# A streaming-encoder trunk on one core: other pads in front of the operands of the products

## The chip, the cores and the metric

The kernel runs on one core of one Trainium2 chip. The metric is the device time of one execution in microseconds (us). The kernel before takes 1405.71 us (median of 3 runs, 1403.22 to 1407.08).

## The reference

Four pre-norm residual layers work on a sequence of 256 tokens of 1024 features. Each has a token mixer and a gated channel mixer; a final RMS norm ends the program.

```python
for i in range(DEPTH):                       # 4
    hn = rmsnorm(h, norm_mix[i])
    if i % 3 == 0:   mix = diff_attention(hn, ...)     # layers 0 and 3
    elif i % 3 == 1: mix = conformer_conv(hn, ...)     # layer 1
    else:            mix = gated_deltanet(hn, ...)     # layer 2
    h = h + mix
    h = h + conv_ffn(rmsnorm(h, norm_ffn[i]), ...)     # every layer
return rmsnorm(h, norm_final)
```

`conv_ffn` multiplies by a 1024 x 5632 matrix, runs a causal convolution of width 3 over the tokens, gates one half with the other, and multiplies by a 2816 x 1024 matrix. All inputs are float32.

## The kernel before

**Layout.** The residual `h` lies feature-major: 128 features of a block on the 128 partitions, 8 blocks of 256 tokens along each partition. All weights of the large products come through one stream, `wst`, in units of 128 x 1024 float32 (512 KB). `Stream.upto` (lines 158 to 178) loads a unit to `wraw` on SyncE's DMA queue, ScalarE casts it to `whi` (line 173) and VectorE puts the remainder into `wlo` (line 174). Both have 4 buffers of 4096 bytes per partition.

**A product in three parts.** A float32 product is made of three products of the faster type `float32r`: high times high, high times low and low times high. `mm3` (lines 282 to 284) and the same three calls in `pair_proj` (lines 298 to 300) issue them:

```python
pe.matmul(o, w[0], x[0], start=start, stop=False)   # L282  hi weights, hi activations
pe.matmul(o, w[0], x[1], start=False, stop=False)   # L283  hi weights, lo activations
pe.matmul(o, w[1], x[0], start=False, stop=stop)    # L284  lo weights, hi activations
```

The second argument is the stationary operand, which TensorE loads first (128 columns, 512 bytes of each partition); the third is the moving operand, streamed through (256 columns, 1024 bytes of each partition). Each product has its own weight load, which runs beside the product before it.

**Which products there are.** The projections of the normed activations move `xh`, `xl` (written in `norm_split`, lines 239 and 240; one block of 256 tokens per step over the 8 blocks): into `psu` in the channel mixers, `pqk` in the attention, `pcu` in the conformer, `pgc` in the delta net. The projections back to the residual move the split activations: `facth`, `factl` in the first three channel mixers, `oh`, `ol` in the attention, `cacth`, `cactl` in the conformer, `goh`, `gol` in the delta net; all go into `acc`. In three places the weights are the moving operand, 512 columns wide, and the activations the stationary one: `pv` (values of the attention), `pz` (gate of the delta net) and the last channel mixer's way back (`acc<-whi,facth`). One small product of the delta net, `pba`, has a stationary operand of 32 columns only (`wA`, `wB`), with `xh`, `xl` moving. Products of plain float32 (the taps of the conformer's convolution into `pcc` at line 712, transposes, the scan of the delta net) are made elsewhere.

**What sets the order.** The order of the work is written out by hand: `attn_order`, `gdn_order` and `ffn_order` list the steps, and the table `WAIT` says how many steps a side chain is put off.

**Where a tile lies.** Tile pools give out the memory of a partition one tile after another, so a tile's place depends on the sizes of those before it. `offset` (line 141) puts an unused tile, a pad of 32n bytes per partition, ahead of the next ones:

```python
def offset(pool, name, n):
    if n:
        pool.tile([P, 8 * n], F32, name="pad" + name, bufs=1)
```

It is called behind `h` in the pool `resid` (line 147, n = AT_X), behind the rope tables in the same pool (line 229, n = -AT_X % 4), in the pool `small` (line 1322, n = 1), and at the head of the pools of the channel mixer (line 397, AT_F), the attention (line 489, AT_A), the conformer (line 668, AT_C) and the delta net (line 818, AT_G). The numbers are

```python
AT_X, AT_F, AT_A, AT_C, AT_G = 3, 2, 1, 1, 1
```

The buffers of one name are whole multiples of 512 bytes apart, and so are the steps within them, so that one number, the place modulo 512 bytes, holds for all products of a kind.

Of the kernel before, what the change touches and what calls it, by code (L numbers as in the profile page):

```python
# [32 lines left out]
PE_TAPS_LAST = 11  # L33
POOL_TAPS = 6
LAG = 2
AT_X, AT_F, AT_A, AT_C, AT_G = 3, 2, 1, 1, 1
MAX_DIAGS = 88
DIAG_STEP = 4
TAIL = 4
# [86 lines left out]
def trunk(ctx: ExitStack, tc: tile.TileContext, xT, pos, wst, wba, params, consts, rows, lamp, nfin, out, layers=None):  # L126
# [5 lines left out]
    resid = ctx.enter_context(tc.tile_pool(name="resid", bufs=1))  # L132
    wpool = ctx.enter_context(tc.tile_pool(name="wpool", bufs=1))
    small = ctx.enter_context(tc.tile_pool(name="small", bufs=2))
# [6 lines left out]
# [4 lines that stand above are left out]
# [81 lines left out]
    rs_bc = resid.tile([P, S], F32, name="rs_bc")  # L226
    rs_tok = resid.tile([P, 32], F32, name="rs_tok")[:, 0:2]
    rope = [resid.tile([P, S], F32, name=f"rope{n}") for n in range(2)]
    offset(resid, "r", -AT_X % 4)
    state = {}  # L230

    def norm_bank(b, gname, goff):
# [1086 lines left out]
        nm, off = names(k + 1)  # L1319
        return lambda b: norm_bank(b, nm, off)  # L1320

    offset(small, "s", 1)
    warm = small.tile([P, P], F32, name="warm", tag="warm", bufs=1)
    ve.memset(warm, 0.0)
    ac.copy(small.tile([P, 1], F32, name="warm1", tag="warm1", bufs=1), warm[:, 0:1])
# [176 lines left out]
```

## Time and profile before

| what | value |
|---|---|
| median of 3 runs | 1405.71 us (1403.22 to 1407.08) |
| the profiled execution, its own time | 1403.77 us |
| its span, first to last instruction | 1401.9 us |
| TensorE busy with products | 1382.7 us, 99% of the span |
| TensorE busy with weight loads | 1311.3 us, 94% |
| VectorE, ScalarE, GpSimd busy | 79%, 63%, 7% |
| granted TensorE clock, mean | 0.997 |
| DMA | 223.94 MB, mean 160 GB/s |

A product's record lasts from when its first column enters to when the last result is out (about 0.28 us for 256 columns), and the next product begins long before that. So the records of neighbours overlap, and the engine's busy share says little. What a product costs is the step from its start to the start of the next one. It is read from the timeline, or by dividing a stretch that holds nothing else by the number of products in it.

### The profile page before, as it was taken

What the parts mean: (1) busy time and instruction counts of PE and PEld (TensorE: products, weight loads), DVE (VectorE), ACT (ScalarE), POOL (GpSimd) and SP (SyncE); (2) the same over time, 40 slices, a digit from 0 to 9 for tenths busy, and PEclk for the clock granted to TensorE, in tenths of its full rate; (3) what the DMA queues carried; (4) which work ended last, traced back from release to release, by engine and by line L of the source; (5) the groups of instructions that cost most, each with busy time, mean ns of one, the idle gap of its engine ahead of it and who ended that gap; (6) DMA issues with size and microseconds to landing.
All of it is one profiled execution on the core that took longest, in us unless ns stands there. A gap on an engine that the chain in (4) does not pass through costs nothing.

```text
span 1401.9 us, 27575 instructions
## 1 busy us (share of the span) xinstructions
PE 1382.7 (99%) x10868; PEld 1311.3 (94%) x10868; DVE 1112.5 (79%) x1994; ACT 877.4 (63%) x1621; POOL 94.1 (7%) x112
## 2 busy tenths in 40 slices
PE   9999999999999999999999999999999999999998
PEld 7889999999889999998998999999999988999996
DVE  7977877788988877787895786787778786887776
ACT  6668965566556555565747765665556576655554
POOL 0010000004530000000100011000000000000000
PEclk9999999999999999999999999999999999999999
DMA  8445666554325666654463333566665544566662
GB/s 278 146 121 165 181 182 183 186 180 129 91 61 170 193 183 183 185 177 133 123 192 93 122 91 121 157 184 187 184 182 180 181 127 134 162 196 185 190 181 91
DMA packets 63138, 223.94 MB, mean 160 GB/s; under 512 B 7200, under 2 KB 8736, under 8 KB 63008
## 3 DMA queue, kind: packets, MB, share of 16 engines
q1 hardware_dynamic: 62720, 221.65, 52.1%
q8 instruction: 85, 1.39, 0.4%
q10 hardware_dynamic: 288, 0.52, 0.1%
q14 instruction: 45, 0.37, 0.1%
HBM read 221.10 MB, written 1.05 MB: 158 GB/s over the span
## 4 chain that ended last, share of the span: by engine, by line
PE 87%; DVE 7%; ACT 3%; issue 1%; POOL 1%; DMA 0%; SPq 0%; POOLq 0%; ACTq 0%; DVEq 0%
PE psu L282 12%; PE psu L284 11%; PE psu L283 11%; PE acc L283 8%; PE acc L282 8%; PE acc L284 8%; PE pcc L712 3%; DVE wlo L174 2%; PE pgc L282 2%; PE pgc L283 2%; PE pgc L284 2%; ACT whi L173 1%; PE pz L282 1%; PE pz L284 1%; PE pz L283 1%
## 5 line engine op out<-in xcount | busy, mean ns | idle before, releaser
L173 ACT CAST whi<-wraw 128x1024 fp32r<-128x1024 f32 (+1 forms) x417 | 435.7, 1047 | 301.3 <-PE psu L283 118.1
L174 DVE TENSOR_TENSOR wlo<-wraw,whi 128x1024 fp32r<-128x1024 f32 (+1 forms) x417 | 509.1, 1222 | 140.9 <-ACT whi L173 132.7
L282 PE MATMUL psu<-xh,whi 128*128 128x256 f32 x1344 | 380.9, 283 | 0.0
L283 PE MATMUL psu<-xl,whi 128*128 128x256 f32 x1344 | 379.3, 282 | 0.0
L284 PE MATMUL psu<-xh,wlo 128*128 128x256 f32 x1344 | 377.2, 281 | 0.0
L284 PEld LDWEIGHTS psu<-xh,wlo 128*128 128x128 f32 x1344 | 255.0, 190 | 0.0
L283 PEld LDWEIGHTS psu<-xl,whi 128*128 128x128 f32 x1344 | 252.7, 188 | 0.3
L282 PEld LDWEIGHTS psu<-xh,whi 128*128 128x128 f32 x1344 | 251.6, 187 | 0.4
L283 PE MATMUL acc<-factl,whi 128*128 128x256 f32 x528 | 147.8, 280 | 0.0
L282 PE MATMUL acc<-facth,whi 128*128 128x256 f32 x528 | 147.5, 280 | 0.0
L284 PE MATMUL acc<-facth,wlo 128*128 128x256 f32 x528 | 146.9, 279 | 0.0
L426 DVE SCALAR_TENSOR_TENSOR fy<-fs,prm,fy 128x255 f32<-128x255 f32 (+1 forms) x352 | 146.4, 477 | 0.0
L422 ACT ACTIVATE fy<-fs,prm 128x256 f32<-128x256 f32 x176 | 96.4, 593 | 7.8 <-DVE fs L418 7.6
L282 PEld LDWEIGHTS acc<-facth,whi 128*128 128x128 f32 x528 | 99.2, 188 | 0.1
L283 PEld LDWEIGHTS acc<-factl,whi 128*128 128x128 f32 x528 | 99.1, 188 | 0.0
L284 PEld LDWEIGHTS acc<-facth,wlo 128*128 128x128 f32 x528 | 98.6, 187 | 0.0
L276 ACT CAST facth<-fa 128x256 fp32r<-128x256 f32 x88 | 35.6, 405 | 90.4 <-DVE fa L430 90.4
L418 DVE TENSOR_TENSOR fs<-psu,rs_bc 128x512 f32<-128x512 f32 x88 | 60.7, 690 | 36.5 <-PE psu L284 36.4
L282 PE MATMUL pqk<-xh,whi 128*128 128x256 f32 x256 | 73.4, 287 | 0.0
L284 PE MATMUL pqk<-xh,wlo 128*128 128x256 f32 x256 | 73.0, 285 | 0.3 <-DVE wlo L174 0.3
L283 PE MATMUL pqk<-xl,whi 128*128 128x256 f32 x256 | 72.9, 285 | 0.0
L282 PE MATMUL pgc<-xh,whi 128*128 128x256 f32 x240 | 69.0, 287 | 0.0
(352 smaller groups left out, 2872.8 us busy)
## 6 DMA issues: line engine op xcount, KB each, us to landing
wraw<-wst SPq DMA_DIRECT2D x415, 512.0 KB, 3.7
h<-xT SPq DMA_DIRECT2D x4, 256.0 KB, 5.4
prm<-params SPq DMA_DIRECT2D x1, 564.0 KB, 7.3
wraw<-wst SPq DMA_DIRECT2D x2, 256.0 KB, 4.3
gain<-nfin SPq DMA_DIRECT2D x1, 512.0 KB, 4.0
out<-fz SPq DMA_DIRECT2D x2, 256.0 KB, 2.0
out<-fz ACTq DMA_DIRECT2D x2, 256.0 KB, 2.5
cst<-consts SPq DMA_DIRECT2D x1, 264.0 KB, 7.0
```

Of the source, the lines that this page charges most:

```text
L173: ac.copy(hi[:, qs], src[:, qs])
L174: ve.tensor_tensor(lo[:, qs], src[:, qs], hi[:, qs].bitcast(F32), ALU.subtract)
L276: state["hi"] = ac.copy(hi, a)
L282: pe.matmul(o, w[0], x[0], start=start, stop=False)
L283: pe.matmul(o, w[0], x[1], start=False, stop=False)
L284: pe.matmul(o, w[1], x[0], start=False, stop=stop)
L418: ve.tensor_tensor(s, ps.rearrange("p (g t) -> p g t", g=2), bc(rs_bc, 2), ALU.mult)
L422: ac.activation(y[:, gv], s[:, gv], AF.Identity, scale=col("ffn_dw", c + 2), bias=col("ffn_dw_b", (i * NP_ + p) * 2 + gv))
L426: ve.scalar_tensor_tensor(y[:, gv, j:], s[:, gv, :S - j], col("ffn_dw", c + 2 - j), y[:, gv, j:], ALU.mult, ALU.add)
L712: pe.matmul(pc[:, 0:S], dg, u[:, j:j + S], start=(n == 0), stop=(n == npe - 1))
```

## The change

Nothing but the pads: their numbers, and two more of them get a name.

```diff
-AT_X, AT_F, AT_A, AT_C, AT_G = 3, 2, 1, 1, 1
+AT_X, AT_R, AT_S, AT_F, AT_A, AT_C, AT_G = 7, 3, 10, 0, 0, 4, 2
...
-    offset(resid, "r", -AT_X % 4)
+    offset(resid, "r", AT_R)
...
-    offset(small, "s", 1)
+    offset(small, "s", AT_S)
```

The instructions and their order on every engine stay as they are; only addresses differ. In the two programs as they are laid out, the operands lie at these places, in bytes modulo 512 within their partition:

| operand | before | after |
|---|---|---|
| `xh`, `xl` | 224 | 352 |
| `facth`, `factl` | 448 | 352 |
| `oh`, `ol` | 416 | 352 |
| `goh`, `gol` | 352 | 352 |
| `cacth`, `cactl` | 288 | 352 |
| weights `whi`, `wlo` | 384 | 64 |
| residual `h` | 128 | 128 |
| taps' input `cu` (three buffers) | 32, 160, 416 | 96, 224, 480 |

The distance "moving less stationary, modulo 512" of the products with 256 columns is thus, before, 352 for `xh` and `xl`, 64 for `fact`, 32 for `o`, 480 for `go`, 416 for `cact`; after, it is 288 for all of them. For the products that move the weights, 512 columns wide, it is 160 before (`pv`, `pz`) and 448 (`acc<-whi,facth`); after, it is 224 for both.

## Rows read from the trace of the kernel before

**Rows 1.** The page: busy us (share of the span), number of instructions.
```profile
PE 1382.7 (99%) x10868; PEld 1311.3 (94%) x10868; DVE 1112.5 (79%) x1994; ACT 877.4 (63%) x1621; POOL 94.1 (7%) x112
```
**Rows 2.** The page: chain that ended last, share of the span by engine.
```profile
PE 87%; DVE 7%; ACT 3%; issue 1%; POOL 1%; DMA 0%; SPq 0%; POOLq 0%; ACTq 0%; DVEq 0%
```
**Rows 3.** Waits of PE alone, longest sums: us in total, times, longest.
```profile
PE poT L621 <- ACT os L617: 2.7, 4, 0.9
PE pat L599 <- DVE pr L591: 1.7, 5, 0.4
```
**Rows 4.** A stretch of a channel mixer, all engines: busy us (count), PEclk, DMA share, GB/s.
```profile
275.41:298.45 23.04, 23.04 (x194) 23.04 (x193) 18.60 (x29) 13.35 (x21) 0.00 (x0) 1.00 0.55 184
```
**Rows 5.** The same stretch, PE on tile psu alone: us, PE busy (products), PEclk.
```profile
275.41:298.45 23.04, 23.04 (x192) 1.00 0.55 184
```
**Rows 6.** Five stretches, PE on tile acc: fact, o, o earlier, go, cact moving.
```profile
298.45:307.75 9.30, 9.30 (x79) 1.00 0.57 174
117.62:124.62 7.00, 7.00 (x62) 1.00 0.59 184
113.82:117.06 3.24, 3.24 (x29) 1.00 0.01 4
890.52:896.67 6.15, 6.15 (x54) 1.00 0.28 89
415.65:429.89 14.24, 14.24 (x122) 1.00 0.45 123
```
**Rows 7.** A stretch of the products with 32 weight columns, PE on tile pba.
```profile
635.73:637.77 2.04, 2.04 (x20) 1.00 0.36 32
```
**Rows 8.** Stretches of products that move 512 columns, PE on acc and pz.
```profile
1377.99:1386.15 8.16, 8.15 (x35) 1.00 0.00 1
...
701.47:712.69 11.22, 11.22 (x48) 1.00 0.63 200
```
**Rows 9.** PE's groups by line and form, one of three lines each: count, busy, mean ns.
```profile
L282 PE MATMUL psu<-xh,whi 128*128 128x256 f32 x1344 | 380.9, 283 | 0.0
...
L282 PE MATMUL acc<-facth,whi 128*128 128x256 f32 x528 | 147.5, 280 | 0.0
...
L282 PE MATMUL pqk<-xh,whi 128*128 128x256 f32 x256 | 73.4, 287 | 0.0
...
L282 PE MATMUL pgc<-xh,whi 128*128 128x256 f32 x240 | 69.0, 287 | 0.0
...
L282 PE MATMUL acc<-oh,whi 128*128 128x256 f32 x128 | 36.9, 291 | 0.0
L282 PE MATMUL acc<-goh,whi 128*128 128x256 f32 x128 | 36.7, 292 | 0.0
...
L282 PE MATMUL pcu<-xh,whi 128*128 128x256 f32 x112 | 32.7, 292 | 0.0
...
L298 PE MATMUL psu<-xh,whi 128*128 128x256 f32 x64 | 18.1, 283 | 0.0
...
L282 PE MATMUL acc<-cacth,whi 128*128 128x256 f32 x64 | 17.6, 283 | 0.0
```
**Rows 10.** The same view: products with 512 moving columns.
```profile
L282 PE MATMUL acc<-whi,facth 128*128 128x512 f32 x88 | 34.7, 396 | 0.0
...
L282 PE MATMUL pz<-whi,xh 128*128 128x512 f32 x64 | 27.0, 422 | 0.0
...
L282 PE MATMUL pv<-whi,xh 128*128 128x512 f32 x64 | 25.9, 412 | 0.3 <-ACT whi L173 0.3
```
**Rows 11.** The chain in order of time: start us, us, what; taps of the convolution.
```profile
339.92 4.33 PE pcc L712 x20
```
**Rows 12.** Timeline of PE in a channel mixer: start us, us, what.
```profile
207.07 0.28 PE L282 MATMUL psu<-xh,whi 128*128 128x256 f32 x1
207.20 0.28 PE L283 MATMUL psu<-xl,whi 128*128 128x256 f32 x1
```

## The prediction

> **What bounds the kernel now.** I begin with the page's busy shares: TensorE's products cover 99% of the span, no other engine more than 79% [rows 1]. A busy share alone proves little here, since the records overlap, so the chain of waits comes next: 87% of it is TensorE [rows 2]. Then the waits of TensorE alone: the longest sum is 2.7 us, the next 1.7 us [rows 3]. TensorE is hardly ever held up by anyone; the time is the sum of its steps, and every nanosecond off a step is off the end, as long as the others keep up. They do: in a stretch of a channel mixer VectorE, which is next, is busy 18.60 of 23.04 us, the DMA share is 0.55, and the clock is granted in full, its upper level of 2.4 GHz [rows 4]. TensorE's part would have to shrink by 19% there before VectorE ruled.
>
> What does a step cost? The stretch of `psu` holds 192 products in 23.04 us, which is 120.0 ns each [rows 5]. The same three-part product has other steps elsewhere. Windows that open in the middle of a run also count the two products still in flight (a record lasts 0.28 us [rows 12]), so two are taken off all of rows 6 but the first: `fact` 9.30/79 = 117.7 ns, `o` 7.00/60 = 116.7 ns, though `o` has an earlier stretch at 3.24/27 = 120.0 ns, `go` 6.15/52 = 118.3 ns, `cact` 14.24/120 = 118.7 ns [rows 6]. Code, sizes, clock and accumulators are alike; what differs between these kinds is the place of the moving operand. And with 32 weight columns instead of 128, but `xh` and `xl` moving from the same place as in `psu`, the step is 2.04/18 = 113.3 ns [rows 7]. So some 6.7 ns of `psu`'s 120.0 belong to the weight load that runs beside it: the two reads hinder each other, and how much depends on how they lie to each other. That is what the change touches.
>
> **The change, part by part.** No instruction is added, removed or moved; no wait and no queue changes. Costs arise only where a read is faster or slower from its new place.
>
> *Products that move `xh`, `xl`.* Three lines times (1344 + 64 + 256 + 240 + 112) = 6048 products [rows 9]; two groups of 16 per line are left out. Now 120.0 ns each, at distance 352. The new distance, 288, is in no row. Bounds: 113.3 ns below (the same stream with a quarter of the weights), 120.0 ns above, as no kind has a higher steady step. Which value? Three readings of the five kinds offer themselves. By the moving operand's own place the twin is `go`, already at 352: 118.3 ns. By the distance, if the pattern repeats every 256 bytes, the twin of 288 is 32, which is `o`: 116.7 ns. By the distance modulo 512 the nearest row is `xh` itself, 64 bytes away: 120.0 ns. The rows don't decide between the last two: by 256 the distances 32, 64, 96, 160, 224 give 116.7, 117.7, 120.0, 118.7, 118.3, by 512 the distances 32, 64, 352, 416, 480 give the same values in the same order, and both curves are smooth. Two readings of three say less than 120.0; I take the middle of the four kinds that aren't `xh`, 117.8 ns: 2.2 ns x 6048 = 13.3 us less.
>
> *Products that move `fact`, `o`, `go`, `cact`.* 1584, 384, 384 and 192 products [rows 9]. At 117.8 ns they change by +0.1, +1.1, -0.5 and -0.9 ns, which is +0.2, +0.4, -0.2, -0.2 us: nothing in sum. Bounds: all at 113.3 ns would take off 4.4 x 1584 + 3.4 x 384 + 5.0 x 384 + 5.4 x 192 = 11.2 us; all at 120.0 ns would add 2.3 x 1584 + 3.3 x 384 + 1.7 x 384 + 1.3 x 192 = 5.8 us.
>
> *Products that move 512 columns of weights.* 3 x (88 + 64 + 64) = 648 [rows 10]. The two distances they have now give 8.16/35 = 233.1 and 11.22/48 = 233.8 ns [rows 8], so place counts for 0.7 ns over them, 0.5 us in sum: nothing. Each holds one weight load like a product of half its length; were that load's share of 6.7 ns to vanish, 4.3 us would go.
>
> *Plain float32 products.* The taps stream 256 columns in 4.33/20 = 216 ns, though their input starts 4 bytes further at every tap [rows 11]: at this slower pace place is not felt. Nothing, either way.
>
> *Writers of the moved tiles.* ScalarE and VectorE write and read at other places too. If that cost them anything, VectorE's 19% of free time in rows 4 hides it.
>
> Sum: 13 us off the profiled execution's 1403.77 us gives 1390.5 us; its time lies 1.9 us under the median of the runs, well within their spread. I say **1390 us**. A difference under 0.3%, some 4.2 us, can't be told from none.
>
> **A rule against the change.** Row first: `psu` and `pba` move the same operand from the same place, and a shorter weight load makes the step 120.0 or 113.3 ns [rows 5, 7]. The Trainium skill's page "SBUF — State Buffer", section "Who interferes with whom", gives TensorE two independent read ports, one for the moving operand and one for the weight load, and says "PE and ACT never wait on anyone". By that rule where operands lie couldn't matter, and the time would stay at 1404 us. The trace disagrees with it as far as those rows go, so I leave it a small chance.
>
> **The rivals.**
>
> *Place is not the cause* (the change does nothing). The five steps could stem from the stages they stand in. For it: `o` has both 116.7 and 120.0 ns at one place [rows 6], so place alone does not fix the step; the start of a run does too. Against it: `psu` keeps 120.0 over 192 products while the `fact` products next to it, in the same stage with the same neighbours, keep 117.7 [rows 5, 6]. It gives 1404 us; 1 in 9.
>
> *The new place is nearly free of hindrance.* At 113.3 ns everything, `xh` gives 6.7 x 6048 = 40.5 us and the rest 11.2 us: 1352 us, or 1348 with the 512 columns. Two thirds of the way down, at 115.2 ns, `xh` gives 4.8 x 6048 = 29.0 us and the rest 2.5 x 1584 + 1.5 x 384 + 3.1 x 384 + 3.5 x 192 = 6.4 us: 1368 us. For it: the step has room down to rows 7, and among five kinds, laid out in five ways, the steps already spread over half of that room. Against it: none of them comes below 116.7. Chance 1 in 4 for anything under 1380 us.
>
> *Slower: all products take `xh`'s step.* The new distance, 288, lies 64 bytes from the worst one, 352, and far from the best ones, 32 and 64. If the pattern repeats every 512 bytes only and is smooth, `fact`, `o`, `go` and `cact` all move towards `xh`. It decides as soon as the step at 288 is above 119.5 ns: then `xh` gains nothing that pays for the 5.8 us that the others lose, and the time is 1410 us. Should the steps go beyond 120.0, each ns costs 6.0 us on `xh` and 2.5 us on the rest; single steps of 125 ns exist (0.13 us within a run whose mean is 120.0 [rows 12]), but no run keeps them. For it: plain nearness. Against it: that curve needs its peak and the fall to 117.7 at 64 in a part no row shows. Chance 1 in 4, most of it between 1408 and 1412 us.
>
> **How the numbers follow.** Forecast, a step of 116.7 to 118.7 ns: 0.39, between 1381 us (20.0 us on `xh`, 2.6 us on the rest) and 1398 us (7.9 us on `xh`, 2.5 us back from the rest). Nearly free: 0.25. Nothing: 0.11. Slower: 0.25. Faster by over 0.3% is therefore 0.64, within 0.3% 0.11, slower 0.25. The range reaches up to 1412 us, all at 120.0 against the median of the runs. Downwards it goes to 1362 us, a step of 114.6 ns for everything: 5.4 x 6048 + 3.1 x 1584 + 2.1 x 384 + 3.7 x 384 + 4.1 x 192 = 40.6 us. Left out are the last ns above the floor, about 0.11, and steps beyond 120.0, about 0.06. The faster cases have a range of their own, 1362 to 1399 us.
>
> **What would show it.** In the profile after, windows of `psu`, `acc` and `pba` like rows 5 to 7: one common step for `psu` and all kinds of `acc`, near 117.8 ns, proves the forecast; 120.0 for all of them the slower rival; the old differences between `psu` and `fact`, unchanged, the rival that place isn't the cause. `pba` should stay at 113.3 and the taps at 216 ns. TensorE's waits should stay under 3 us each; a wait for `wlo` on TensorE's list would mean that VectorE took over, and I would be wrong about the cover. I am also wrong if the time moves while the steps do not.

## The result, and the profile after

The changed kernel takes 1388.79 us (median of 4 runs, 1386.96 to 1390.58), the kernel before, run beside it, 1404.47 us (4 runs, 1401.76 to 1407.08). The ratio is 0.9888, with a 95% interval of 0.9863 to 0.9914. That is 16 us off; 1390.0 us had been forecast. The profiled execution took 1386.96 us.

From its page: the span; the busy times, as in [rows 1]; and the shares of the chain, as in [rows 2].

```profile
span 1385.1 us, 27575 instructions
...
PE 1363.5 (98%) x10868; PEld 1292.5 (93%) x10868; DVE 1110.9 (80%) x1994; ACT 879.9 (64%) x1621; POOL 94.9 (7%) x112
...
PE 84%; DVE 9%; ACT 4%; POOL 1%; issue 1%; DMA 0%; SPq 0%; POOLq 0%; ACTq 0%; DVEq 0%
```

The counts are the old ones. TensorE lost 19.2 us of busy time, VectorE and ScalarE kept theirs within 3 us: only the products became quicker. The chain still belongs to TensorE, with 84% where it had 87%, and VectorE has two per cent more.

Now the steps. Windows of the profile after, PE on one tile at a time (us, products, clock, DMA share, GB/s): `psu`; then `acc` with `fact`, `o`, `go` and `cact` moving; then `pba`, `pz`, and the last channel mixer's way back, where 512 columns of weights move. They answer to [rows 5 to 8].

```profile
271.46:293.39 21.93, 21.93 (x190) 1.00 0.59 188
...
1058.23:1067.10 8.87, 8.87 (x78) 1.00 0.60 178
...
116.58:123.35 6.76, 6.76 (x60) 1.00 0.58 170
...
881.30:887.30 6.01, 6.01 (x53) 1.00 0.29 91
...
409.98:424.22 14.23, 14.23 (x124) 1.00 0.42 125
...
625.44:627.76 2.32, 2.32 (x22) 1.00 0.24 53
...
691.24:701.74 10.50, 10.50 (x46) 1.00 0.63 187
...
1361.26:1368.73 7.46, 7.46 (x33) 1.00 0.01 3
```

Each of these windows opens inside a run, so two products still in flight are taken off (one at 512 columns): 21.93/188 = 116.7 ns, 8.87/76 = 116.7, 6.76/58 = 116.6, 6.01/51 = 117.8, 14.23/122 = 116.6, 2.32/20 = 116.0, 10.50/45 = 233.3, 7.46/32 = 233.1. A window is exact to about one product (0.6 ns at 190 of them, 2 ns at 60). The starts in the timeline tell more closely: over all clean stretches of a kind, the first six steps or so of each run left out (a run has to settle, see below), the means are these, to 0.1 ns; the columns for the experiments are used further down:

| step in ns, start to start | before | after | moving alone | weights alone | distance 112 or 368 |
|---|---|---|---|---|---|
| `xh`, `xl` into `psu` | 120.0 | 116.7 | 118.3 | 117.7 to 118.3 (all of `xh`) | 113.5 |
| `fact` | 117.8 | 116.7 | 118.3 | 118.6 | 113.4 |
| `o` | 117.3 | 116.7 | 118.3 | 120.0 | 114.0 |
| `go` | 118.3 | 117.0 | 118.3 | 117.0 | 113.9 |
| `cact` | 118.7 | 116.7 | 118.3 | 118.3 | |
| `pba` (32 weight columns) | 113.4 | 116.4 | 114.9 | | |

Five kinds with five different steps have become one step, at 116.7 to 117.0 ns, as the common distance would have it.

The cover held. All engines in the stretch of `psu` (PE, weight loads, VectorE, ScalarE, GpSimd), as in [rows 4]:

```profile
271.46:293.39 21.93, 21.93 (x190) 21.93 (x189) 18.13 (x29) 13.30 (x20) 0.00 (x0) 1.00 0.59 188
```

VectorE is busy 18.13 of 21.93 us, 83% where it was 81%. The waits of TensorE (sum, times, longest) answer to [rows 3]; the longest sum went from 2.7 to 2.9 us, and no wait for `wlo` is among the three:

```profile
PE poT L621 <- ACT os L617: 2.9, 4, 0.9
PE pat L599 <- DVE pr L591: 2.3, 5, 0.6
PE psu L299 <- DVE xl L240: 1.9, 3, 1.0
```

**What was given back.** The measured steps would give 3.3 x 6048 = 20.0 us on `xh`, 1.1 x 1584 = 1.7 on `fact`, 0.6 x 384 = 0.2 on `o`, 1.3 x 384 = 0.5 on `go`, 2.0 x 192 = 0.4 on `cact`: 23 us. The span lost 16.8. I added up the time from each product's start to the next, by kind, in both traces. `psu` gave 13.2 us of 14.1 that its 4224 products could; `pqk` 1.1 of 2.6; and `pgc` became 0.6 us longer, where its 768 products should have given 2.6. Part of that are gaps: what the steps over 0.14 us hold beyond the usual step grew, over all the kinds in the table but `pba`, from 27.2 to 29.9 us.

`pgc` met the clock. Two windows of the profile after, all engines (the granted clock is the third column from the right); the first window's own group of `pgc`, one line of three; and two neighbours of it in the timeline:

```profile
734.60:741.43 6.83, 6.83 (x51) 6.77 (x48) 0.73 (x1) 6.09 (x9) 0.00 (x0) 0.50 0.22 72
...
748.25:755.08 6.83, 6.83 (x80) 6.06 (x78) 1.12 (x4) 3.76 (x7) 0.00 (x0) 0.50 0.38 116
...
L282 PE MATMUL pgc<-xh,whi 128*128 128x256 f32 x8 | 3.5, 436 | 0.0
...
738.27 0.41 PE L284 MATMUL pgc<-xh,wlo 128*128 128x256 f32 x1
738.48 0.41 PE L282 MATMUL pgc<-xh,whi 128*128 128x256 f32 x1
```

The kernel before has one such window, in the same phase of the delta net, the blocks of the triangular solve:

```profile
757.70:764.50 6.80, 6.74 (x35) 5.04 (x34) 2.56 (x7) 3.25 (x7) 0.00 (x0) 0.50 0.35 121
```

In these windows the clock is at its lower level, 1.2 GHz; what TensorE did before the first were small products of 32 x 32 (`py`). Twenty-four products of `pgc` fell into that window. One step took 380 ns and the others 213.3, so they cost 2.5 us more than at 116.7 ns, most of the 3.2 us that `pgc` lacks. A later execution of the same changed kernel (the last experiment) has the low clock in the same places for half as long, a mean of 0.75 in either window:

```profile
734.60:741.43 6.83, 6.83 (x80) 6.70 (x78) 0.02 (x1) 6.67 (x10) 0.00 (x0) 0.75 0.27 79
...
748.25:755.08 6.83, 6.83 (x75) 5.57 (x72) 2.60 (x7) 3.30 (x7) 0.00 (x0) 0.75 0.35 119
```

That execution took 1384.73 us, 2.2 us less. So a part of what was given back differs from one execution to the next.

At the start, where `pqk` stands, TensorE isn't alone on the path. The first 60 us of the kernel before, and then of the kernel after, all engines:

```profile
0.00:60.00 60.00, 57.17 (x372) 47.94 (x373) 51.25 (x105) 39.55 (x78) 4.61 (x8) 1.00 0.67 221
```

```profile
0.00:60.00 60.00, 56.41 (x380) 47.90 (x381) 52.00 (x106) 40.55 (x82) 5.32 (x9) 1.00 0.67 221
```

The same 221 GB/s flow in, VectorE is busy 52 of 60 us, and the quicker products got only eight further. In the chain of this stretch, VectorE's `wlo` holds the largest share of any line, 14.8% before and 13.0% after; ScalarE's `whi` went from 3.2% to 5.0%. By the chain, a quicker product there waits for other engines, those that prepare the weights first.

### The profile page after: what moved, and what is told of

Its sections match the earlier page's. It is cut to its first block, busy times and chain, and to the rows that moved or that the text cites. A ratio compares the mean times of both kernels' runs of the same rounds, so it can differ in the third digit from the quotient of the medians.

```text
span 1385.1 us, 27575 instructions
## 1 busy us (share of the span) xinstructions
PE 1363.5 (98%) x10868; PEld 1292.5 (93%) x10868; DVE 1110.9 (80%) x1994; ACT 879.9 (64%) x1621; POOL 94.9 (7%) x112
## 4 chain that ended last, share of the span: by engine, by line
PE 84%; DVE 9%; ACT 4%; POOL 1%; issue 1%; DMA 0%; SPq 0%; POOLq 0%; ACTq 0%; DVEq 0%
PE psu L282 11%; PE psu L283 11%; PE psu L284 11%; PE acc L282 8%; PE acc L283 8%; PE acc L284 8%; DVE wlo L174 3%; PE pgc L282 2%; PE pcc L712 2%; PE pgc L283 2%; PE pgc L284 2%; ACT whi L173 2%; PE pz L282 1%; PE pz L283 1%; PE pz L284 1%
## 5 line engine op out<-in xcount | busy, mean ns | idle before, releaser
L282 PE MATMUL psu<-xh,whi 128*128 128x256 f32 x1344 | 375.9, 280 | 0.0
L283 PE MATMUL psu<-xl,whi 128*128 128x256 f32 x1344 | 375.2, 279 | 0.0
L418 DVE TENSOR_TENSOR fs<-psu,rs_bc 128x512 f32<-128x512 f32 x88 | 60.7, 690 | 27.5 <-PE psu L284 26.8
```

The source lines that it names most:

```text
L418: ve.tensor_tensor(s, ps.rearrange("p (g t) -> p g t", g=2), bc(rs_bc, 2), ALU.mult)
```

## The experiments

Three theories stood at the outset. **A, the distance**: moving less stationary place sets the step, and nothing else does (with a period of 512 or of 256 bytes). **B, the moving operand's own place** sets it. **C, the weights' own place** sets it. In each diff the removed line is that of the changed kernel.

### The moving operands alone, the weights alone

```diff
-AT_X, AT_R, AT_S, AT_F, AT_A, AT_C, AT_G = 7, 3, 10, 0, 0, 4, 2
+AT_X, AT_R, AT_S, AT_F, AT_A, AT_C, AT_G = 7, 13, 1, 15, 15, 3, 1
```

All moving operands lie at 352 as in the changed kernel, the weights at 384 as before: distance 480 for all.

> All moving operands at 352, the weights back at 384 (distance 480 for all). Theory A, the distance modulo 512 alone sets the step: all kinds take the step that go had at distance 480 in the kernel before, 118.3 ns; psu goes from 120.0 to 118.3, and the time to about 1405 - 10 + 2 = 1397 us. Theory B, the moving operand's own place sets it: 116.7 ns for all, as in the changed kernel, 1389 us. Theory C, the weights' place sets it: no gain on psu, 120.0 ns, 1405 us or more.

Measured: 1398.10 us (7 runs, 1395.52 to 1401.96) against 1405.17, ratio 0.9949 (0.9931 to 0.9967). The windows of `psu` and `fact`:

```profile
274.77:297.02 22.25, 22.25 (x190) 1.00 0.58 190
...
297.49:306.49 9.00, 9.00 (x78) 1.00 0.52 177
```

22.25/188 = 118.35 ns and 9.00/76 = 118.4 ns, and all other kinds but `pba` the same within 0.1 (table above). This is the step that `go` had in the kernel before, at the same distance of 480. Half of the gain, one step for all.

```diff
-AT_X, AT_R, AT_S, AT_F, AT_A, AT_C, AT_G = 7, 3, 10, 0, 0, 4, 2
+AT_X, AT_R, AT_S, AT_F, AT_A, AT_C, AT_G = 3, 7, 1, 12, 11, 11, 11
```

The weights lie at 64 as in the changed kernel, the moving operands where they were before. The distances are 160 for `xh`, 384 for `fact`, 352 for `o`, 288 for `go`, 224 for `cact`.

> The weights at 64, all moving operands where the kernel before had them. Distances: xh 160, fact 384, o 352, go 288, cact 224. Theory A (distance modulo 512): o takes the 120.0 ns that xh had at 352, go the 116.7 ns of the changed kernel, the others are new. Theory A with a period of 256: xh takes cact's 118.7, o 120.0, cact go's 118.3, go 116.7. Theory B (own place): every kind as in the kernel before, psu 120.0, fact 117.8, time 1405 us. Theory C (the weights' place): all at 116.7 ns, time 1389 us.

Measured: 1396.48 us (4 runs, 1394.06 to 1397.88), ratio 0.9934 (0.9908 to 0.9960). `psu`, `fact`, `o` and `go`:

```profile
274.72:296.78 22.06, 22.06 (x190) 1.00 0.59 191
...
297.25:306.26 9.02, 9.02 (x78) 1.00 0.55 177
...
118.30:125.25 6.95, 6.95 (x60) 1.00 0.60 174
...
886.12:892.12 6.01, 6.01 (x53) 1.00 0.29 87
```

22.06/188 = 117.3, 9.02/76 = 118.7, 6.95/58 = 119.8, 6.01/51 = 117.8 ns. By the starts, the runs of 96 and 192 products of `psu` keep 117.3 ns in layers 0 to 2 and 118.7 in layer 3: already here one distance, 160, shows two steps. The weights all lie at one place, and the kinds still differ: C falls. `go` moves from 352 in all four kernels; its mean step is 118.3 ns at distance 480 (twice) and 117.0 at distance 288 (twice): B falls as well. And `o`, put at distance 352, took over the 120.0 ns that `xh` had there. A stands.

### Both moved together, and the 512 or 256 bytes

```diff
-AT_X, AT_R, AT_S, AT_F, AT_A, AT_C, AT_G = 7, 3, 10, 0, 0, 4, 2
+AT_X, AT_R, AT_S, AT_F, AT_A, AT_C, AT_G = 11, 3, 1, 9, 9, 13, 11
```

Moving operands at 480, weights at 192: both 128 further, the distance of 288 kept.

> Moving operands at 480, weights at 192: the distance stays 288, both places are moved by 128. Theory A (distance): 116.7 ns for all kinds and 1389 us, as in the changed kernel. Theories B and C (one place alone): another step, most likely between 117 and 120 ns. If the place within 512 bytes of either operand counts beside the distance, the step also differs from 116.7.

Measured: 1391.91 us in a single run. `psu` and `cact`:

```profile
273.63:295.77 22.14, 22.14 (x190) 1.00 0.58 189
...
412.38:426.62 14.24, 14.24 (x124) 1.00 0.43 127
```

`cact` has 14.24/122 = 116.7 ns, and `pqk`, `o` and `go` have 116.7 to 117.0. But `fact` has a mean of 117.7, and `psu` shows 22.14/188 = 117.8 ns here and in all its runs of 96 and 192 products in layers 0 to 2, and 116.7 in those of layer 3, with both operands at the same places. So the distance carries over in most kinds, and something besides the places can hold a whole run at another value. The scan of entries below shows such a thing at distance 192; at 288 it was not tried.

```diff
-AT_X, AT_R, AT_S, AT_F, AT_A, AT_C, AT_G = 7, 3, 10, 0, 0, 4, 2
+AT_X, AT_R, AT_S, AT_F, AT_A, AT_C, AT_G = 7, 9, 1, 3, 3, 7, 5
```

Moving operands at 352, weights at 256: distance 96 for all. With a period of 256, 96 is the twin of 352, the bad one; with a smooth curve over 512 bytes it would lie near the good ones.

> Moving operands at 352, weights at 256: distance 96, which is xh's old 352 less 256. Theory A with a period of 256: 120.0 ns for all kinds, about 1410 us. Theory A with a period of 512: a new distance, next to fact's 64 (117.8 ns), so about 117 to 119 ns and 1393 to 1400 us. Theory B (own place): 116.7 ns, 1389 us.

Measured: 1410.69 us in a single run, beside 1405.17. The window of `psu`:

```profile
276.30:298.86 22.56, 22.56 (x190) 1.00 0.57 187
```

22.56/188 = 120.0 ns, and all other kinds the same, `pba` too. That speaks for a period of 256 bytes. This kernel is also the slower rival of the prediction, made real at another distance: all products at 120.0 ns, 1410.69 us in this one run, where the rival's arithmetic gave 1410.

### A scan of the distance

The changed kernel gets products ahead of its work: one plain float32 product, then 72 products of 256 columns, all on zeros, for each distance; zeros do not enter the output.

```diff
...
+for d in range(0, 512, 16):
+    run(P + d // 4, 0, 72, P)           # run(moving, stationary, count, weight columns)
+for d in (32, 96, 160, 224):
+    run(3 * P + d // 4, 2 * P, 72, P)   # both 1024 bytes further
+    run(P + 24 + d // 4, 24, 72, P)     # both 96 bytes further
+for cols in (32, 64, 96):
+    for d in (32, 96, 160, 224):
+        run(P + d // 4, 0, 72, cols)
```

> The changed kernel with a scan of extra products ahead of its work (their results are not used): runs of 72 products of 256 columns with 128 weight columns, both operands in one tile, at distances 0 to 496 in steps of 16 bytes; then the distances 32, 96, 160 and 224 with both operands moved by 1024 or 96 bytes; then the same distances with 32, 64 and 96 weight columns. Theory A with a period of 256: the second half of the scan repeats the first, about 120.0 ns at 96 and 352, 116 to 118 at 32 and 288, 118 to 119 at 160 and 416, 118 at 224 and 480, whichever place the operands have; distances in between show whether a step under 116.7 ns exists. If the hindrance comes from the weight load, 32 columns give a smaller step at every distance, down to about 113 ns. Theory B (one place alone counts): a curve that follows the moving operand's place, and shifts when both are moved by 96 bytes.

Measured: the last 24 products of seven runs, PE on the scan's tile, at the distances 32, 96, 112, 192, 288, 352 and 368; then distance 96 with both 96 bytes further; then distance 32 with only 32 weight columns.

```profile
29.28:32.08 2.80, 2.80 (x26) 1.00 0.03 6
...
64.36:67.23 2.88, 2.88 (x26) 1.00 0.00 0
...
72.94:75.66 2.72, 2.72 (x26) 1.00 0.03 6
...
116.46:119.17 2.72, 2.72 (x26) 1.00 0.00 0
...
168.80:171.60 2.80, 2.80 (x26) 1.00 0.00 0
...
203.88:206.75 2.88, 2.88 (x26) 1.00 0.00 0
...
212.46:215.18 2.72, 2.72 (x26) 1.00 0.00 0
...
316.97:319.84 2.88, 2.88 (x26) 1.00 0.00 0
...
360.51:363.32 2.81, 2.81 (x26) 1.00 0.02 6
```

Divided by 24: 116.7, 120.0, 113.3, 113.3, 116.7, 120.0, 113.3, 120.0 and 117.1 ns. The lasting steps of one period, from the starts in the timeline:

| distance | 0 | 16 | 32 | 48 | 64 | 80 | 96 | 112 |
|---|---|---|---|---|---|---|---|---|
| ns | 120.0 | 118.7 | 116.7 | 118.3 | 117.8 | 120.0 | 120.0 | **113.3** |
| **distance** | **128** | **144** | **160** | **176** | **192** | **208** | **224** | **240** |
| ns | 118.5 | 118.6 | 118.6 | 119.3 | **113.3** | 119.2 | 118.3 | 117.3 |

From 256 on, the same sixteen values come again, one by one. Moving both operands by 96 or by 1024 bytes leaves the step within 1.2 ns of the table's (at 160; at 32, 96 and 224 it is the same). That is A with a period of 256 bytes, with nothing else of the kernel beside it: same code, same zeros, no writers. The curve isn't smooth: 112 lies next to one of the worst places and is one of the two best. Each value belongs to one way into a run, the same for all.

The narrower loads give a second answer. With 32 weight columns the four distances measured 117.3, 117.5, 117.8 and 117.5 ns, with 64 columns 119.0, 116.7, 117.1 and 116.7, with 96 columns 116.7, 117.8, 116.7 and 116.7. A load of a quarter of the length evens the distances out; it doesn't take 6.7 ns away. That reading of `pba` in the prediction falls.

### The best distances in the kernel, and the worst

```diff
-AT_X, AT_R, AT_S, AT_F, AT_A, AT_C, AT_G = 7, 3, 10, 0, 0, 4, 2
+AT_X, AT_R, AT_S, AT_F, AT_A, AT_C, AT_G = 7, 6, 1, 6, 6, 10, 8
```

Distance 192 for all (352 and 160).

> Moving operands at 352, weights at 160: distance 192, at which the scan's run stood at 113.3 ns. Theory A with a period of 256: 113.3 ns for every kind of product with 256 columns, 3.3 ns under the changed kernel's, which over some 8700 products is 29 us less: 1360 us; part of it may come back where TensorE then waits for casts or loses clock, so up to 1367 us. Rival: the scan holds only for undisturbed runs over one and the same pair of operands, and in the kernel, where operands change with every product, steps stay near 117 ns and the time near 1389 us. Second rival: steps fall to 113.3, but VectorE and ScalarE no longer keep up, and over 10 us come back as waits of TensorE.

Measured: 1375.07 us (5 runs, 1373.25 to 1379.69) against 1403.97, ratio 0.9802 (0.9781 to 0.9822). A stretch of `psu` in layer 0, and the like in layer 3:

```profile
273.50:295.63 22.14, 22.14 (x190) 1.00 0.60 188
...
1331.80:1353.11 21.30, 21.30 (x190) 1.00 0.57 187
```

That is 117.8 and 113.3 ns. All the runs of 96 and 192 products of `psu` in layers 0 and 1 keep 117.8 ns, and those in layers 2 and 3 keep 113.3. One distance, two steps.

```diff
-AT_X, AT_R, AT_S, AT_F, AT_A, AT_C, AT_G = 7, 3, 10, 0, 0, 4, 2
+AT_X, AT_R, AT_S, AT_F, AT_A, AT_C, AT_G = 7, 14, 1, 14, 14, 2, 0
```

Distance 448 (352 and 416), the twin of 192.

> Moving operands at 352, weights at 416: distance 448, which is 192 plus 256. Theory A with a period of 256: the same as with distance 192, 113.3 ns and 1360 to 1367 us. With a period of 512 only: another step.

Measured: 1375.75 us (4 runs), ratio 0.9824 (0.9786 to 0.9862), but spread from 1367.45 to 1386.45 us. In the profiled execution, `psu` in the same mixer, and the 512 columns at the end:

```profile
267.99:289.30 21.30, 21.30 (x190) 1.00 0.59 193
...
1341.38:1348.02 6.64, 6.64 (x30) 1.00 0.04 14
```

21.30/188 = 113.3 ns this time (`fact` too, but 115.2 for `go` and 115.5 for `pcu`, whose runs fall on both values), and 6.64/29 = 229 ns where 233 stood. A spread of 19 us over four runs fits a step that takes one of two values from run to run, but one execution was profiled, so the other three aren't shown.

```diff
-AT_X, AT_R, AT_S, AT_F, AT_A, AT_C, AT_G = 7, 3, 10, 0, 0, 4, 2
+AT_X, AT_R, AT_S, AT_F, AT_A, AT_C, AT_G = 7, 12, 1, 0, 0, 4, 2
```

Distance 0 (352 and 352).

> Moving operands and weights both at 352: distance 0, at which the scan's run stood at 120.0 ns. Theory A: 120.0 ns for every kind, about 1410 us, as with distance 96. If the kernel's products did not follow the scan: something else.

Measured: 1408.50 us in a single run beside 1403.97. `psu`, and the 512 columns at the end:

```profile
276.31:298.87 22.56, 22.56 (x190) 1.00 0.58 187
...
1383.18:1390.45 7.27, 7.27 (x33) 1.00 0.01 2
```

120.0 ns for every kind, but 7.27/32 = 227 ns for 512 columns: one of the worst distances for the one width is the best seen for the other. It cannot pay: at 6.6 ns off 648 products it is 4.3 us.

### Why one distance has two steps

The same extra products again, this time with a lead: 0 to 7 products at another distance (64 or 0) go ahead of 60 at 112 or 192. Behind them stand runs of 512 columns.

```diff
...
+for d in (112, 192):
+    for other in (64, 0):
+        for lead in range(8):
+            run(d, 60, S, lead, other)
+for d in (0, 32, 64, 96, 112, 128, 144, 160, 192, 224):
+    run(d, 36, 2 * S)
```

> The changed kernel with extra products ahead of its work (results not used): runs of 60 products at distance 112 and at 192, each entered after 0 to 7 products at distance 64, and after 0 to 7 at distance 0; then runs of 36 products with 512 moving columns at ten distances. If the lasting step depends on how a run is entered, the runs at 192 fall into two groups, 113.3 and 117.8 ns; if 112 is free of that, all of its runs stand at 113.3. If neither depends on the entry, every run stands at 113.3 and the two states in the kernel have another cause. The products with 512 columns: 226.7 ns at 0, 233.3 at 32 and 224 (as 288 and 480 gave), 228.9 at 64, 233 to 234 at 96 and 160.

Measured: the last 24 products at 112 after no lead; at 192 after no lead (twice, in the block of leads at 64 and in that at 0), after three products at 64, and after one at 0.

```profile
9.82:12.54 2.72, 2.72 (x26) 1.00 1.03 398
...
129.78:132.61 2.83, 2.83 (x26) 1.00 0.03 6
...
190.38:193.21 2.83, 2.83 (x26) 1.00 0.00 0
...
152.21:154.93 2.72, 2.72 (x26) 1.00 0.00 0
...
197.66:200.38 2.72, 2.72 (x26) 1.00 0.00 0
```

At 112 all 16 runs end at 2.72/24 = 113.3 ns. At 192 nine end at 113.3 and seven at 117.8, and they stay there. The run without a lead gave 117.8 both times; a lead of three at either distance gave 113.3, and so did one at 0, but not one at 64. So at these two distances the distance decides which steps can last, and the way into a run which of them it is. Of 512 columns, distance 0 gives 226.7 ns, 64 and 192 give 229 and 233, 112 231, the others 233 to 234.5.

### The best version

Distance 112 needs 16 bytes, which a pad of 32n can't give. Every moving tile is made 256 bytes longer and used from its fifth element on; the weights lie at 256. The distances are 112 or, where a buffer stands behind one that grew by 256 bytes, 368.

```diff
-AT_X, AT_R, AT_S, AT_F, AT_A, AT_C, AT_G = 7, 3, 10, 0, 0, 4, 2
+AT_X, AT_R, AT_S, AT_F, AT_A, AT_C, AT_G = 7, 9, 1, 3, 3, 7, 5
...
-    xh = resid.tile([P, KC, S], F32R, name="xh")
+    xh = resid.tile([P, KC * S + 64], F32R, name="xh")[:, 4:4 + KC * S].rearrange("p (k t) -> p k t", k=KC)
...
```

(The same for `xl`, `fact`, `cact`, `o`, `go`.) The numbers are those of the kernel at distance 96, which took 1410.69 us; the 16 bytes, and the longer tiles that they need, are the whole difference.

> All moving operands 16 bytes further in their tiles, so that every distance is 112 or 368 (112 modulo 256), the other place at which the scan stood at 113.3 ns. If a distance has one lasting step, the whole kernel takes 113.3 ns and some 1360 to 1367 us. If, as with 192 and 448, a run can also last at 117.8 ns, the time lies between those and 1386 us and differs from run to run. If the period is 512 for 112: half of the products, those at 368, take another step.

Measured: **1366.67 us** (5 runs, 1364.93 to 1369.32) against 1403.54, ratio 0.9740 (0.9724 to 0.9756). `psu` and `fact`, and the page's chain:

```profile
268.69:290.00 21.30, 21.30 (x190) 1.00 0.60 189
...
290.45:298.95 8.50, 8.50 (x77) 1.00 0.62 188
...
PE 74%; DVE 14%; ACT 5%; issue 4%; POOL 2%; DMA 0%; SPq 0%; POOLq 0%; ACTq 0%; DVEq 0%
```

21.30/188 = 113.3 and 8.50/75 = 113.3 ns, in layer 0 as in the others. Its steps (table above) would give 6.5 x 6048 = 39.3 us on `xh`, 4.4 x 1584 = 7.0 on `fact`, 3.3 x 384 = 1.3 on `o` and 4.4 x 384 = 1.7 on `go`, 49 us; 37 came. VectorE has 14% of the chain now, twice its share before: the cover wears thin. The missing 12 us can be found by adding up the starts as above: over the kinds that moved, the steps over 0.14 us hold 8.7 us more than in the kernel before (36 against 27), and some 5 us are shorter steps above 113.4 ns, in which runs still settle. `pqk` fares worst, with 1.1 us of the 5.0 that its 768 products could give; `psu` gives 24.9 of 27.5.

### The changed kernel again

An unchanged copy, to see what varies between executions.

> The changed kernel once more, on the same chip as the others: 1389 us and 116.7 ns again. If its steps, too, could last at another value, such as the 117.8 ns that distance 288 showed with both operands moved by 128 bytes, some runs would lie some 8 us higher.

Measured: 1388.07 us (4 runs, 1384.73 to 1389.55), ratio 0.9887 (0.9869 to 0.9904). `psu` and `pba`:

```profile
272.16:294.09 21.93, 21.93 (x190) 1.00 0.59 188
...
626.17:628.44 2.27, 2.27 (x22) 1.00 0.14 16
```

`psu` repeats its 116.7 ns. `pba` has 2.27/20 = 113.5 ns where the first execution had 116.0: one kernel, no place changed, two steps.

## Why the prediction was right

**The bound.** TensorE's steps were to be the time. They were: the steps fell, the rest stayed, and the time followed. The rule that was set against it, no influence of place, does not hold. The scan runs the same products on the same zeros at 113.3 to 120.0 ns by distance alone. The Trainium skill's page "SBUF — State Buffer", section "Who interferes with whom", says that TensorE's moving and weight reads use independent ports and wait on no one; these runs disagree with what the prediction drew from it, that place can't matter, by 6.7 ns a product and, between the kernels at distances 96 and 112, by 44 us. They don't show where in the engine or the memory the time goes.

**The size on `xh`.** Forecast 117.8 ns, measured 116.7: the term of 13.3 us was 20 us by its steps, of which some 14.5 us came (`psu` 13.2, `pqk` 1.1, `pcu` 0.9, `pgc` 0.6 the other way). Of the three readings, the distance with a period of 256 bytes was the right one, and it alone said 116.7. I had taken a middle between a reading that was right and two that weren't. The smooth curve over 512 bytes falls by distance 96 (120.0 ns); the moving operand's own place falls by `go`, which changed its step without moving. What the forecast had too little, the give-back of 6 us took away again; that the median lies 1.2 us from the forecast is in part two errors that cancel, which is luck.

**The other kinds.** They were put at nothing, with 117.8 ns for all; they went to 116.7 to 117.0 ns, which is 2.8 us. The 512 columns were put at nothing: by its windows `pz` went from 233.8 to 233.3 ns, which would be 0.2 us over 384 products, and the last way back stayed at 233.1.

**The floor.** "Some 6.7 ns of `psu`'s 120.0 belong to the weight load" is the step of the argument that failed. With 32, 64 or 96 weight columns the scan finds no step under 116.7 ns, and `pba` went from 113.4 to 116.4 ns in one execution and not in the other. `pba`'s 113.3 varies between executions of one kernel, so it isn't the price of a shorter load. The number 113.3 was nonetheless the lowest lasting step seen, so the bound drawn from it stood: by luck, not by its reason. What holds of that paragraph is its second half, that the step depends on how the two operands lie to each other.

**The rivals.** *Place is not the cause* had `o`'s two values at one place for it. That observation was right: a distance can hold two steps, as 192 does (and 160 and 288 above). The conclusion wasn't. *Nearly free of hindrance* was right that such a place exists, at 112 and at 192, and wrong that 288 is one. *Slower* was a real outcome of a real distance, 96, and its price of 1410 us was met within a microsecond by the one run; the place from which it was argued, 64 bytes from the worst one, says nothing, since 112 lies 16 bytes from a worst one.

**The cover and the taps.** VectorE had 17% left in the stretch of `psu` and no wait for `wlo` came up as a large one; the taps kept their pace (36.5 us in all before, 36.6 after).

**What stays open.** Why the period is 256 bytes, and why 112 and 192 are the good ones, no run tells: the distance is shown as the cause, the thing in the memory or the engine that makes it one is not. Nor is it shown which property of the entry selects the step at 192. The entry was varied at 112 and 192 alone, so other distances of the scan's table may hold a second step that it doesn't show.

## What to carry to other kernels

Where products follow each other without a gap and each loads its own weights, measure the step from start to start per kind of product; if kinds of one shape differ, compare the distance between moving and stationary operand modulo 256 bytes before looking at code. A scan of 32 short runs finds the good distances in one execution, and a good one should be tried with several ways into it: one that settled the same way every time (112 here, in 16 of 16) is worth more than one that sometimes does. Expect less than step times count, as stretches in which other engines prepare the weights give little back (here the first 60 us).

## What the runs showed of the hardware that was not expected

- Sixteen bytes decide 44 us: distance 96 gives 120.0 ns a product and 1410.69 us, distance 112 gives 113.3 ns and 1366.67 us, with the same table of pads (one run and a median of five, beside 1405.17 and 1403.54 us for the kernel before).
- A run of equal products at one distance can settle at either of two steps, 113.3 or 117.8 ns at 192, and keep it for whole channel mixers.
- Settling at 112 took between 1 and some 17 products, in the scans and in the kernel, and at 192 at most 10 in the scans; a short run, such as `pba`'s 24 products, shows its entry as well as its place.
- At the lower clock the distance isn't felt: where 13 or more products of `pgc` fell into it, they stepped by 213 ns at distances 0, 96, 160, 192, 288, 448 and 480 alike.
- The best distance for 256 columns isn't the best for 512: at 0, 256 columns take 120.0 ns, as slow as any, and 512 take 226.7, the fastest seen; at 112 they take 113.3 and 231.
- No lasting step came below 113.3 ns. The Trainium skill's page "TensorE: Matmul & The Clock Gate", section "Wait — 56ns, not 53.3ns?", gives columns over 2.4 GHz and some 2.5 ns, by which an estimate for 256 columns is 109.2 ns; no run here reached it, and none shows what the difference is.
